# mLSTM as three rounded passes, rounded local-branch weights by casting transfers, and the gates' rows in the first branch gate's projection

## The chip, the core and the metric

The kernel runs on one core of a Trainium2 chip. A time is the device time of one launch in microseconds; the figure for a kernel is the median of its runs. Before the change it is 880.17 us, the median of three runs that lie between 879.93 and 880.27. The profile is that of one further execution, taken by the hardware profiler.

## The reference, cut to what matters

One decoder layer for 512 tokens of width 1024, all inputs float32. On one normalised input it computes an mLSTM branch (4 heads, keys of 128, values of 256) and a sliding-window attention branch ("local branch"), each multiplied by its own branch matrix, weighed by its own sigmoid gate and added; then an output projection, an MLP, a gated embedding and a last norm.

```python
proj = h @ w_in
qk_ml, v_ml, o_ml, if_pre, q_sw, k_sw, v_sw, g_a, g_b = jnp.split(proj, split_idx, axis=-1)
qk_ml = silu(causal_depthwise_conv(qk_ml, conv_qk))
...
log_d = where(causal, b[t] - b[s] + ic[s], -inf)      # b: running sum of the log forget gate
m_t = maximum(inter, max(log_d))
scores = einsum("bhtk,bhsk->bhts", qc, kc) * exp(log_d - m_t)
num = w_inter * (C @ qc) + einsum("bhts,bhsv->bhtv", scores, vc)
den = w_inter * (n @ qc) + sum(scores)
h = num / maximum(abs(den), exp(-m_t))
...
y_a = sigmoid(o_ml) * h_ml
merged = sigmoid(g_a) * (y_a @ w_branch_a) + sigmoid(g_b) * (y_b @ w_branch_b)
x = x + merged @ w_out
```

The kernel computes the mLSTM for the whole sequence at once: for a head it forms the 512 x 512 lower triangle of `scores` in 128 x 128 blocks (four key blocks `s`, four query blocks `t`, ten pairs with `s <= t`) and multiplies it by the values, with a column of ones beside the values so that the row sum `den` falls out of the same product.

## The kernel before, in words

TensorE (`T`, PE in the profile) is given float32 data in two ways. Most products are split: an operand `x` is rounded to float32r (`hi`, a copy on ScalarE, L137), the rest `x - hi` is subtracted on VectorE (`lo`, L138), and a product is three rounded passes, hi·hi, hi·lo and lo·hi (`pairs`, L163, issued by `chain`, L171). The products of the mLSTM are instead given plain float32 operands, one call each: `ml_scores` (L819) and `ml_out` (L831).

The stages around the change, in order of time in the profile:

- The v projection (`by_tokens(w_vml, ...)`, L530, about 44 to 83 us), then the o projection (L592, to about 123 us). Each is done by `seven` (L438), a form with seven products of quarter matrices instead of eight, whose results come out of PSUM by `post` under the names p1, c11, t21, t22, c22, c12, c21. `put_v` (L517) writes v, with a one in column 256 of each head, to the four `vm` tiles; `put_o` stores sigmoid(o) to DRAM (`god`, on POOL's queue).
- The gates' rows (L536 to L578): from the 8 gate preactivations of every token, as rows of 4 x 512, the running sums and maxima on VectorE with three activations on ScalarE (`lf`, `mst`, `fl`, `rr`, `gg`, `em`). `rr` is stored to DRAM (L554) and read back, one row per head broadcast over 128 partitions (`rows`, L565), both on POOL's queue; 14 small transposes on PE (L572, L574) turn `gg` and `em` into columns, which five copies bring to `gc`. In the program all this stands between the v and the o projection.
- The two branch gates (`gate_proj`, L596; w_gb about 123 to 165 us, w_ga to about 204 us), each as two halves `j`, each half by `seven`; results go to DRAM (`gd`) on POOL's queue. The remaining q, the mLSTM's q and k (`qk_proj`, `silu`) and the attention (`swa_probs`, `swa_out`) follow, to about 325 us.
- The mLSTM itself (about 325 to 400 us): for each head `ml_decay` (exponentials on ScalarE), `ml_scores`, `ml_out`, `ml_norm`; between them `branch_b(i)`, eight products of 24 matmuls with the weights `w_b`, and at the end `ya_of`, transposes and splits into the `ya` tiles. Then `merge` multiplies `ya` by `w_a`.

A weight is loaded raw by a transfer on SP's queue (L152), then rounded and subtracted (`load_w`, L155); `wh` and `wl` have four buffers each. Tiles of one tag share a fixed number of buffers: 34 of 512 columns ("act"), two of the big form that `h`, `ya` and `x1` take one after the other ("big"), four of 1024 columns ("lm"). The order of the instructions of each engine is not the written order: a planner places an instruction when its inputs and buffers are there by its own model of the costs, and takes the one written first where several could go. `tc.issue_after(x)` keeps what follows behind instruction `x`.

Of the kernel before, what the change touches and what calls it, by code (L numbers as in the profile page):

```python
# [16 lines left out]
P = 128  # L17
S = 512
# [18 lines left out]
def block_kernel(  # L37
# [82 lines left out]
    def tk(n):  # L120
        return tp_.tile([P, NH * (DV + 1)], F32, tag="tk", bufs=4, name=nm(n))
# [33 lines left out]
    def load_w(src, n, dims, raw=None):  # L155
# [4 lines left out]
        split(parts, raw[:, :n])  # L160
        return [q.rearrange("p (k c) -> p k c", k=dims) for q in parts]
# [317 lines left out]
    for m in range(NT):  # L479
        t = tk("vm").rearrange("p (h d) -> p h d", h=NH)  # L480
        G.memset(t[:, :, DV : DV + 1], 1.0)
        vm.append(t)

# [32 lines left out]

    def put_v(m, nh, ps, k):  # L517
        o = vm[m][:, 2 * nh : 2 * nh + 2, :DV]
        src = ps.rearrange("p (h d) -> p h d", h=2)
# [10 lines left out]
    by_tokens(w_vml, post_by_tokens(put_v), True)  # L530

# [8 lines left out]
    lf = row("lf")[:4, :]  # L540
    V.scalar_tensor_tensor(lf, fg, -1.0, fg, ALU.mult, ALU.max)
    A.activation(lf, lf, AF.Exp, scale=-1.0)
    A.activation(lf, lf, AF.Ln, bias=1.0)
    V.scalar_tensor_tensor(lf, fg, 0.0, lf, ALU.min, ALU.subtract)
    mst = act_f("mst")[:4, :]
    V.tensor_tensor_scan(mst, lf, ig, 0.0, ALU.add, ALU.max)
    fl = row("fl")[:4, :]
    for c in range(NT):
        V.tensor_tensor_scan(fl[:, c * P : (c + 1) * P], lf[:, c * P : (c + 1) * P], zeros4, 0.0, ALU.add, ALU.add)
    rr = act_f("rr")[:4, :]  # L550
    V.tensor_sub(rr, fl, mst)

    rrd = dp.tile([NH, 512], F32, name="rrd")
    nc.gpsimd.dma_start(out=rrd, in_=rr)  # L554
    gg = [act_f("gg")[:4, :] for _ in range(NT)]
    for t in range(NT):
        sl = slice(t * P, (t + 1) * P)
        V.tensor_sub(gg[t][:, sl], ig[:, sl], fl[:, sl])
        if t:
            V.tensor_scalar_add(gg[t][:, : t * P], gg[t - 1][:, : t * P], fl[:, t * P - 1 : t * P])  # L560
    em = act_f("em")[:4, :]
    A.activation(em, mst, AF.Exp, scale=-1.0)
    rows = [row("row") for _ in range(NH)]
    for h in range(NH):
        nc.gpsimd.dma_start(out=rows[h], in_=rrd[h : h + 1, :].broadcast_to([P, 512]))  # L565

    pgc = pg[:, :512]
    with tc.issue_after(last_mm[0].ins):
        for t in range(NT):
            for s in range(t + 1):  # L570
                c = (t * NT + s) * 4
                T.transpose(pgc[:, c : c + 4], gg[t][:, s * P : (s + 1) * P], ident[:4, :4])  # L572
            c = (NT * NT + t) * 4
            T.transpose(pgc[:, c : c + 4], em[:, t * P : (t + 1) * P], ident[:4, :4])  # L574
    gc = c1.tile([P, NT * NT + NT, 4], F32, name="gc")
    for t in range(NT):
        V.tensor_copy(gc[:, t * NT : t * NT + t + 1, :], pgc[:, t * NT * 4 : (t * NT + t + 1) * 4].rearrange("p (a b) -> p a b", b=4))
    V.tensor_copy(gc[:, NT * NT :, :], pgc[:, NT * NT * 4 : (NT * NT + NT) * 4].rearrange("p (a b) -> p a b", b=4))  # L578


# [15 lines left out]
    def gate_proj(wd):  # L596

        out_d = [None] * 4
        for j in range(2):
# [21 lines left out]
            def post(what, ps):  # L621
                new = lambda: act_f(what).rearrange("p (n c) -> p n c", n=2)
                if what == "p1":
                    keep["p1"] = new()
                    A.copy(keep["p1"], ps)  # L625
                elif what[0] == "t":
                    keep[what] = new()
                    add(keep[what], ps, keep["p1"])
                else:
                    half, nh = int(what[1]), int(what[2]) - 1  # L630
                    o = res[nh][:, :, 256:] if half == 1 else res[nh][:, :, :256]
                    if what != "c11":
# [3 lines left out]
                    A.activation(o, ps, AF.Sigmoid)  # L636
# [17 lines left out]
    gbd = gate_proj(w_gb)  # L654
# [118 lines left out]
    qk_proj(7)  # L773

    for h in range(NH):
        silu(h)
        silu(4 + h)


# [8 lines left out]
    def ml_decay(h):  # L788
        pr = rows[h]
        dg = act_f("dg")  # L790
        V.tensor_tensor(
            dg.rearrange("p (t j) -> p t j", t=NT),
            pr.rearrange("p (t j) -> p t j", t=NT),
            tri.unsqueeze(1).broadcast_to([P, NT, P]),
            ALU.add,
        )
        wT = []
        for s in range(NT):
            dm = act_f("dm")
            for t in range(s, NT):  # L800
                src = dg if t == s else pr
                A.activation(
                    dm[:, t * P : (t + 1) * P],
                    src[:, t * P : (t + 1) * P],
                    AF.Exp,
                    bias=gc[:, t * NT + s, h : h + 1],
                )
            wT.append(dm)
        wts[h] = wT

    def ml_scores(h):

        two, one = ps_a(), ps_t()
        banks = [two[:, :512], two[:, 512:], one, two[:, 512:]]
        at = [0, 0, 0, 384]
        for s in (0, 1, 3, 2):
            n0 = s * P
            psc = banks[s][:, at[s] : at[s] + S - n0]
            T.matmul(psc, qk[4 + h][:, n0 : n0 + P], qk[h][:, n0:], start=True, stop=True, skip_group_check=True)  # L819
        for s in range(NT):  # L820
            n0 = s * P
            dm = wts[h][s]
            V.tensor_mul(dm[:, n0:], banks[s][:, at[s] : at[s] + S - n0], dm[:, n0:])

    def ml_out(h):
        wT = wts.pop(h)
        for half in (1, 0):
            pn = ps_a().rearrange("p (n c) -> p n c", n=2)
            for t in (2 * half, 2 * half + 1):
                for s in range(t + 1):  # L830
                    last_mm[0] = T.matmul(  # L831
                        pn[:, t % 2, : DV + 1], wT[s][:, t * P : (t + 1) * P], vm[s][:, h, :], start=s == 0, stop=s == t, skip_group_check=True
                    )
# [26 lines left out]
    def branch_b(i):  # L860
        ps = ps_g()
        mm_T(ps, load_w(w_b[i], KT * P, KT), yb)
# [3 lines left out]

    _, ya = big_hl("ya")
# [24 lines left out]
    for h in range(NH):  # L892
        branch_b(NH + h)
        ya_of(h)

# [542 lines left out]
```

## Time and profile before

| | |
|---|---|
| median of three runs | 880.17 us |
| the profiled execution | 879.82 us, with a span of 878.0 us |
| instructions in the span | 11545, of them 4372 matmuls |
| granted TensorE clock | 0.998 of full |
| HBM | 91.30 MB read, 8.40 MB written |
| transfers | SP's queue 93.15 MB, POOL's queue 12.59 MB |

Busy times are sums of an engine's instructions. Matmuls overlap in the pipeline, so the mean length of one in a group (389 ns at 512 columns) is longer than the step from one to the next; a step is read from the chain of waits, which gives the time of so many matmuls in a row. In a group, "out<-in" names the tiles, and the shape is partitions x elements. "wr", "wh", "wl" are weights raw, rounded and rest; "ps.." are PSUM tiles; "SPq" and "POOLq" are the sequencers that issue transfers.

### The profile page before, as it was taken

Reading aid. Unit: us, or ns where it says so; the run is one execution under the profiler, and the core shown is the slowest. Engines: PE = TensorE matmul, PEld = TensorE weight load, DVE = VectorE, ACT = ScalarE, POOL = GpSimd, SP = SyncE. Lnnn points to the kernel's source line nnn. Section 1 sums busy time; section 2 is a strip of 40 time slices with the busy share of each in tenths; the row PEclk is TensorE's granted clock in tenths of the full one; section 3 lists DMA queues with packets and bytes.
Section 4 is the critical chain, followed back from the end, with each engine's and each line's share of the span. In section 5 each row is a group of like instructions: output and inputs, shape, how many; then the busy total and the mean of one; then the engine's idle time right before and its main releaser. Section 6 shows DMA issues by size and latency. Waiting matters only on the chain.

```text
span 878.0 us, 11545 instructions
## 1 busy us (share of the span) xinstructions
PE 866.8 (99%) x4372; PEld 725.6 (83%) x4372; DVE 657.2 (75%) x966; ACT 483.5 (55%) x803; POOL 34.1 (4%) x58
## 2 busy tenths in 40 slices
PE   8999999999999999999999999999999999999996
PEld 7888889998777777788888888888888888888886
DVE  6999887875789876665896669756956794698557
ACT  6684554544676768743344665356435634564843
POOL 1111010000000000000020000000000000020000
PEclk9999999999999999999999999999999999999999
DMA  7765244435122162274244612530352054125302
GB/s 266 211 180 186 73 150 169 165 111 196 52 73 72 49 199 88 97 240 144 72 75 145 236 49 71 197 106 10 124 185 75 1 186 149 49 52 141 121 0 96
DMA packets 32793, 106.74 MB, mean 122 GB/s; under 512 B 4573, under 2 KB 4573, under 8 KB 32738
## 3 DMA queue, kind: packets, MB, share of 16 engines
q1 hardware_dynamic: 27570, 93.15, 31.2%
q0 software_dynamic: 5024, 12.59, 5.9%
q8 instruction: 34, 0.56, 0.3%
q10 hardware_dynamic: 144, 0.26, 0.1%
q14 instruction: 21, 0.17, 0.1%
HBM read 91.30 MB, written 8.40 MB: 114 GB/s over the span
## 4 chain that ended last, share of the span: by engine, by line
PE 90%; DVE 4%; ACT 3%; DMA 2%; issue 1%; SPq 0%; ACTq 0%; DVEq 0%
PE psg L171 50%; PE psp L171 23%; PE psa L171 7%; PE pst L171 4%; PE psa L831 1%; PE pst L747 1%; DVE wl L138 1%; DMA wr<-in_w_vsif 1%; ACT lm L712 1%; PE psa L819 1%; PE psa L689 1%; PE psa L690 1%; ACT wh L137 0%; DMA wr<-in_w_gb 0%; PE psp L980 0%
## 5 line engine op out<-in xcount | busy, mean ns | idle before, releaser
L137 ACT CAST wh<-wr 128x1024 fp32r<-128x1024 f32 x138 | 144.8, 1051 | 180.3 <-PE psg L171 74.8
L138 DVE TENSOR_TENSOR wl<-wr,wh 128x1024 fp32r<-128x1024 f32 x138 | 167.8, 1219 | 85.9 <-ACT wh L137 84.6
L171 PE MATMUL psg<-x,wh 128*128 128x512 f32 x512 | 157.7, 389 | 0.0
L171 PE MATMUL psp<-wh,uf 128*128 128x512 f32 x448 | 138.6, 389 | 0.0
L171 PEld LDWEIGHTS psg<-x,wh 128*128 128x128 f32 x512 | 96.0, 188 | 19.9
L171 PE MATMUL psg<-x,wl 128*128 128x512 f32 x256 | 99.6, 389 | 0.0
L171 PEld LDWEIGHTS psp<-wh,uf 128*128 128x128 f32 x448 | 84.1, 188 | 17.5
L171 PE MATMUL psp<-wl,uf 128*128 128x512 f32 x224 | 87.2, 389 | 0.0
L171 PE MATMUL psg<-h,wh 128*128 128x512 f32 x256 | 81.1, 395 | 0.7 <-DVE rc L715 0.7
L137 ACT CAST wh<-wd 128x1024 fp32r<-128x1024 f32 x44 | 46.2, 1052 | 54.0 <-PE psp L171 21.9
L138 DVE TENSOR_TENSOR wl<-wd,wh 128x1024 fp32r<-128x1024 f32 x44 | 53.1, 1217 | 14.7 <-ACT wh L137 14.5
L171 PEld LDWEIGHTS psg<-x,wl 128*128 128x128 f32 x256 | 48.0, 188 | 10.0
L171 PEld LDWEIGHTS psg<-h,wh 128*128 128x128 f32 x256 | 47.0, 188 | 11.2 <-issue 1.6
L171 PE MATMUL psg<-h,wl 128*128 128x512 f32 x128 | 50.5, 395 | 0.0
L138 DVE TENSOR_TENSOR uf<-F,uf 128x1792 fp32r<-128x1792 f32 (+2 forms) x20 | 33.0, 1652 | 21.8 <-ACT uf L137 21.8
L171 PEld LDWEIGHTS psp<-wl,uf 128*128 128x128 f32 x224 | 42.0, 188 | 8.7
L171 PE MATMUL psg<-yb,wh 128*128 128x512 f32 x128 | 41.3, 402 | 0.1
L171 PE MATMUL psg<-ya,wh 128*128 128x512 f32 x128 | 39.5, 390 | 0.0
L137 ACT CAST uf<-F 128x1792 fp32r<-128x1792 f32 (+2 forms) x20 | 27.9, 1396 | 20.5 <-DVE F L1133 20.4
L1157 DVE SCALAR_TENSOR_TENSOR xk<-psp,r,xk 128x512 f32<-128x512 f32 x48 | 33.7, 744 | 5.5 <-PE psp L171 5.2
L171 PE MATMUL psg<-hS,wh 128*128 128x256 f32 x192 | 35.6, 284 | 0.0
L171 PE MATMUL psa<-h,wh 128*128 128x256 f32 x192 | 35.3, 285 | 0.2 <-ACT p L625 0.2
(322 smaller groups left out, 1745.6 us busy)
## 6 DMA issues: line engine op xcount, KB each, us to landing
wr<-in_w_up SPq DMA_DIRECT2D x32, 512.0 KB, 3.3
wd<-in_w_down SPq DMA_DIRECT2D x24, 512.0 KB, 3.7
wr<-in_w_qsw SPq DMA_DIRECT2D x8, 512.0 KB, 4.3
gd<-gr POOLq DMA_DIRECT2D x8, 512.0 KB, 3.7
wr<-in_w_qkml SPq DMA_DIRECT2D x8, 512.0 KB, 3.2
wr<-in_w_b SPq DMA_DIRECT2D x8, 512.0 KB, 3.2
gl<-gd SPq DMA_DIRECT2D x8, 512.0 KB, 3.4
wr<-in_w_a SPq DMA_DIRECT2D x8, 512.0 KB, 4.4
```

The source lines that it names most:

```text
L137: A.copy(dst[0], src)
L138: last_low[0] = V.tensor_sub(dst[1], src, r32(dst[0]))
L171: last_mm[0] = T.matmul(ps, l, r, start=first and i == 0, stop=last and i == len(ops) - 1, skip_group_check=parts)
L689: T.matmul(o, q[:, n * P : (n + 1) * P], kk[kp][ab][:, k0 : k0 + 256], start=True, stop=False)
L690: T.matmul(o, q[:, n * P : (n + 1) * P], kl[kp][ab][:, k0 : k0 + 256], start=False, stop=True)
L712: A.activation(lm3[:, g, :], lm3[:, g, :], AF.Exp, bias=nmx[:, g : g + 1], scale=0.125, accum_out=sm[:, g : g + 1])
L747: T.matmul(o[HALF[ab], :], v[:, c : c + 64], w[:, ab * 512 : (ab + 1) * 512], start=j == 0, stop=j == len(terms) - 1)
L819: T.matmul(psc, qk[4 + h][:, n0 : n0 + P], qk[h][:, n0:], start=True, stop=True, skip_group_check=True)
L831: last_mm[0] = T.matmul(pn[:, t % 2, : DV + 1], wT[s][:, t * P : (t + 1) * P], vm[s][:, h, :], start=s == 0, stop=s == t, skip_group_check ...
L1157: V.scalar_tensor_tensor(o, ps[:, t, :], r2[:, 2 * toks + t : 2 * toks + t + 1], o, ALU.mult, ALU.add)
```

## The change

In the mLSTM every product becomes three rounded passes. `vm` holds rounded v, with two columns of ones per head (258 columns); the rest of v goes to DRAM (`vld`, eight stores on POOL's queue) and is read back per head on SP's queue. q and k of a head and its weights `wT` are split on ScalarE and VectorE into the slots of the `ya` tiles, taken in turn (`spare`). Scores of the last key block are computed over 256 columns, of which 128 are used. The 128 x 512 tiles of weights per head become three of 512, 384 and 256 + 128 columns. `ya`'s tiles are taken earlier, and head 0's decay is written ahead of `qk_proj(7)`. The eight branch products stand two ahead of head 0's outputs, one ahead of each later head's, one between head 2's outputs and head 3's scores, and two at the end.

`branch_b` gets its rounded weights by a second transfer from DRAM that casts, on POOL's queue; the rest is still a subtraction on VectorE.

The gates' rows are computed in the first branch gate's projection: `gates` is called where the first half's t22 is read, `gate_columns` where the second half's c11 is read.

```diff
-        return tp_.tile([P, NH * (DV + 1)], F32, tag="tk", bufs=4, name=nm(n))
+        return tp_.tile([P, NH * (DV + 2)], F32, tag="tk", bufs=4, name=nm(n))
...
+        if cast:
+            nc.gpsimd.dma_start(out=parts[0], in_=src)
+            last_low[0] = V.tensor_sub(parts[1], raw[:, :n], r32(parts[0]))
+        else:
+            split(parts, raw[:, :n])
...
+        A.copy(t[:, :, DV:], ones[:, : 2 * NH].rearrange("p (h d) -> p h d", h=NH))
...
+    def store_low():
+        for o, t in kept:
+            nc.gpsimd.dma_start(out=o, in_=t)
+        kept.clear()
+
     def put_v(m, nh, ps, k):
+        if k is not None:
+            store_low()
         o = vm[m][:, 2 * nh : 2 * nh + 2, :DV]
+        two = lambda t: t.rearrange("p (h d) -> p h d", h=2)
+        low = act_r("vl")
         if k is None:
-            A.copy(o, src)
+            A.copy(o, two(ps))
+            V.tensor_sub(two(low), two(ps), r32(o))
         else:
-            V.tensor_add(o, src, k.rearrange("p (h d) -> p h d", h=2))
+            V.tensor_add(k, ps, k)
+            A.copy(o, two(k))
+            V.tensor_sub(two(low), two(k), r32(o))
+        kept.append((vld[:, 2 * nh : 2 * nh + 2, m, :], two(r32(low))))
...
+    def gates():
+        lf = row("lf")[:4, :]
...
+    def gate_columns():
+        pgc = ps_t()
...
             def post(what, ps):
+                for work in beside.pop((j, what), ()):
+                    work()
...
-    gbd = gate_proj(w_gb)
+    gbd = gate_proj(w_gb, {(0, "t22"): [gates], (1, "c11"): [gate_columns]})
...
+    ya_parts, ya = big_hl("ya")
+    def spare():
+        k = turn[0] % KT
+        turn[0] += 1
+        return [t[:, k, :] for t in ya_parts]
+    def qk_parts(h):
+        for i in (h, 4 + h):
+            hl = spare()
+            split(hl, qk[i])
+            qk[i] = hl
...
     def ml_scores(h):
+        psc = [two[:, :512], two[:, 512:896], one[:, :256], one[:, 256:]]
+        q, k = qk[h], qk[4 + h]
         for s in range(NT):
+            n0 = min(s, 2) * P
+            ops = pairs([t[:, s * P : (s + 1) * P] for t in k], [t[:, n0:] for t in q])
+            for j, (l, r) in enumerate(ops):
+                T.matmul(psc[s], l, r, start=j == 0, stop=j == 2, skip_group_check=True)
+        for j, n in enumerate((512, 384, 384)):
+            for s in ((0,), (1,), (2, 3))[j]:
+                V.tensor_mul(wT[s], psc[s][:, P:] if s == 3 else psc[s], wT[s])
+            hl.append([t[:, :n] for t in spare()])
+            split(hl[j], dm[j][:, :n])
...
     def ml_out(h):
+        low = sp.tile([P, NT, DV], F32R, tag="lm", bufs=LMB, name=nm("vl"))
+        nc.sync.dma_start(out=r32(low), in_=vld[:, h])
...
+                    T.matmul(o, hi, vm[s][:, h, :], start=s == 0, stop=False, skip_group_check=True)
+                    T.matmul(o[:, :DV], hi, low[:, s, :], start=False, stop=False, skip_group_check=True)
+                    last_mm[0] = T.matmul(o, lo, vm[s][:, h, :], start=False, stop=s == t, skip_group_check=True)
...
-        mm_T(ps, load_w(w_b[i], KT * P, KT), yb)
+        mm_T(ps, load_w(w_b[i], KT * P, KT, cast=True), yb)
...
     ml_decay(0)
+    qk_proj(7)
+    silu(0)
+    silu(4)
+    qk_parts(0)
     ml_scores(0)
+    for h in range(1, NH):
+        silu(h)
+        silu(4 + h)
     rds = []
+    todo = list(range(KT))
     for h in range(NH):
-        branch_b(h)
+        for _ in range(1 if h else 2):
+            branch_b(todo.pop(0))
         if h + 1 < NH:
             ml_decay(h + 1)
+            qk_parts(h + 1)
         with tc.issue_after(last_mm[0].ins):
             rds.append(ml_out(h))
         if h + 1 < NH:
+            if h == 2:
+                branch_b(todo.pop(0))
             with tc.issue_after(last_mm[0].ins):
                 ml_scores(h + 1)
...
     for h in range(NH):
-        branch_b(NH + h)
+        if h % 2 == 0:
+            branch_b(todo.pop(0))
         ya_of(h)
```

More of the change, by code (lines that the diff above doesn't have):

```diff
@@ L153, in load_raw, with load_w @@
         return raw
-    def load_w(src, n, dims, raw=None):
+    def load_w(src, n, dims, raw=None, cast=False):
         if raw is None:
@@ L530, in block_kernel @@
     by_tokens(w_vml, post_by_tokens(put_v), True)
+    store_low()
     def row(n):
@@ L539, in block_kernel @@
     V.tensor_copy(fg, pgf[:4, :])
[L540 to L578, printed above, removed]
     god = dp.tile([P, NH, NT, DV], F32, name="god")
@@ L771, in block_kernel @@
             swa_out(*units[u][:2])
[L773 to L777, printed above, removed]
+    ya_parts, ya = big_hl("ya")
+    turn = [0]
+    def spare():
[7 more added lines that the diff above has]
+            qk[i] = hl
     hs = [[act_f("hs") for _ in range(2)] for _ in range(NH)]
@@ L796, in ml_decay @@
         )
-        wT = []
+        dm = [act_f("dm") for _ in range(3)]
+        wT = [dm[0], dm[1][:, :384], dm[2][:, :256], dm[2][:, 256:384]]
         for s in range(NT):
-            dm = act_f("dm")
             for t in range(s, NT):
```

70 lines of the change are left out of this document (49 added, 21 removed).

## The prediction

> **What bounds the kernel now.** I read the page's busy shares first, then the chain of waits in order of time, then busy time by stretches.
>
> ```profile
> PE 866.8 (99%) x4372; PEld 725.6 (83%) x4372; DVE 657.2 (75%) x966; ACT 483.5 (55%) x803; POOL 34.1 (4%) x58
> PE 90%; DVE 4%; ACT 3%; DMA 2%; issue 1%; SPq 0%; ACTq 0%; DVEq 0%
> 60.00:95.00 35.00, 35.00 (x165) 28.69 (x164) 34.86 (x50) 19.71 (x22) 3.44 (x6) 1.00 0.51 170
> 95.00:128.00 33.00, 32.83 (x169) 28.03 (x168) 25.45 (x27) 17.36 (x21) 4.98 (x7) 1.00 0.36 128
> 128.00:165.00 37.00, 37.00 (x307) 36.69 (x306) 29.98 (x37) 17.44 (x21) 1.63 (x3) 1.00 0.43 152
> 165.00:204.00 39.00, 39.00 (x321) 38.48 (x320) 29.29 (x36) 19.47 (x24) 2.13 (x4) 1.00 0.44 155
> 325.00:400.00 75.00, 74.72 (x341) 60.44 (x340) 48.99 (x103) 51.93 (x116) 0.00 (x0) 1.00 0.44 148
> ```
>
> The last five rows give stretch, length, then busy time of PE, PEld, DVE, ACT and POOL, the granted clock, DMA share and GB/s. PE is busy throughout at full clock, and 90% of the chain is PE. So a pass of TensorE that disappears is worth its own length, unless an engine that feeds PE now comes late. Those feeders are loaded unevenly: VectorE is full from 60 to 95, where the v projection ends and the o projection begins (34.86 of 35.00 us), has 7.55 us free in the rest of the o projection, 7.0 in the first branch gate's, 26 in the mLSTM stretch.
>
> **The change part by part. First the PE passes.** These pieces of the chain (start, length, what, how many) price every form of matmul that the change touches:
>
> ```profile
> 357.85 4.33 PE psa L831 x20
> 366.75 1.72 PE psa L819 x6
> 362.19 0.43 PE pst L819 x2
> 133.70 2.88 PE psa L171 x24
> 21.28 5.79 PE psg L171 x48
> 386.88 5.46 PE psg L171 x24
> L831 PE MATMUL psa<-vm,dm 128*128 128x257 f32 x80 | 18.1, 380 | 0.0
> L171 PE MATMUL psg<-wh,h 128*128 128x264 f32 x64 | 13.0, 296 | 0.0
> ```
>
> The code multiplies 40 pairs of blocks at L831 and four per head at L819; the group shows 80, the chain 6 + 2 per head. An unrounded product is therefore two instructions: 4.33/20 = 0.217 us each at 257 columns. A rounded product is one: 2.88/24 = 0.120 us at 256 columns, 5.79/48 = 0.121 at 264, 5.46/24 = 0.228 at 512.
>
> Outputs: per head 10 pairs, now three instructions of 258, 256 and 258 columns, 30 x 0.121 = 3.62 us for 4.33. Scores: before 1.72 + 0.43 = 2.15 us per head. After, three passes over 512, 384, 256 and 256 columns (the last block is widened from 128). The 384-column rounded form is not in the trace; it lies between 0.120 and 0.228, and I take the midpoint 0.174, since cost grows evenly with columns between those rows. 3 x (0.228 + 0.174 + 0.120 + 0.120) = 1.93 us, by the ends 1.76 and 2.09. Saved: 0.71 + 0.22 = 0.93 us per head, **3.7 us for four heads** (3.1 to 4.4 by those ends).
>
> The Trainium skill, FP8 and Floating Point Precision, section TensorE Precision Notes, says that true FP32 takes four passes through the array. Read as three passes for four, 17.3 us of outputs would fall by 4.3 and 8.6 us of scores, with the wider block, by 1.5: 5.8 us, 874.4 as the time. The trace has each pass dearer when it is its own instruction (0.120 us against half of 0.217), so I keep 3.7.
>
> **Second, VectorE and ScalarE in the mLSTM.**
>
> ```profile
> L138 DVE TENSOR_TENSOR wl<-wr,wh 128x1024 fp32r<-128x1024 f32 x138 | 167.8, 1219 | 85.9 <-ACT wh L137 84.6 <-PE psg L171 0.8
> L137 ACT CAST wh<-wr 128x1024 fp32r<-128x1024 f32 x138 | 144.8, 1051 | 180.3 <-PE psg L171 74.8 <-PE psp L171 53.0 <-issue 20.9
> L138 DVE TENSOR_TENSOR ms<-ms,ms 128x512 fp32r<-128x512 f32 x8 | 5.3, 684 | 0.5 <-ACT ms L137 0.5
> L137 ACT CAST ms<-ms 128x512 fp32r<-128x512 f32 x8 | 4.8, 620 | 7.1 <-DVE ms L923 7.1
> L823 DVE TENSOR_TENSOR dm<-psa,dm 128x384 f32<-128x384 f32 x4 | 2.2, 550 | 0.2 <-ACT dm L802 0.2
> L676 DVE SCALAR_TENSOR_TENSOR acc<-acc,sg 128x512 f32<-128x512 f32 x8 | 5.0, 683 | 0.0
> 327.01 1.28 ACT L675
> 330.35 1.88 PE psg L171 x7
> 334.38 4.58 PE psg L171 x20
> 374.18 5.49 PE psg L171 x24
> PEld psa L819 <- DVE hd L835: 0.6, 1, 0.6
> ```
>
> Each head gets five new splits: q and k (512), and weights of 512, 384 and 384. VectorE: 3 x 0.684 + 2 x 0.550 = 3.15 us, 12.6 in all; ScalarE about 3 x 0.62 + 2 x 0.50 = 2.9 us, 11.4 in all, against 8 x 1.051 = 8.4 us of casts of `w_b` that go to transfers. Between 325 and 400 VectorE becomes 48.99 + 12.6 = 61.6 of 75 - 3.7 = 71.3 us (86%), ScalarE 51.93 + 3.0 = 54.9. Neither is full, so the cover is the eight products of `branch_b`, 5.46 us each, that PE runs between heads. The latency, though, grows: from a score to its use there is now a copy and a subtraction more, 0.62 + 0.68 = 1.3 us. Two heads get two products in front, two get one; with one product the 5.46 us must hold multiplications (1.9 us as before), splits (1.78 on VectorE), and other VectorE work. If the cover is gone the price is 1.3 us per head. The entry is tight as well: rounded q and k of head 0 go into slots of the normalised input's tiles, free only when `qk_proj(7)` has been read. The serial piece behind it is table load 1.28, two sigmoids, as long as a cast, and two products (0.683 each, together 2.6), splits (2.0), scores 1.9, products and splits of the weights (4.5): 12.3 us against two branch products and the scores, 2 x 5.46 + 1.9 = 12.8 us. Bounds: 0 to 4 x 1.3 = 5.2 us, or a gain of up to 0.6 us (a weight load of L819 that waited for an eviction, the last row above); taken 0.5. At the end two branch products, 10.9 us, still cover head 3's normalisation, which took 6.5 us from its last matmul (374.18) to its end (380.65, quoted below).
>
> **Third, transfers.**
>
> ```profile
> wr<-in_w_b SPq DMA_DIRECT2D x8, 512.0 KB, 3.2
> xk<-q POOLq DMA_DIRECT2D x6, 256.0 KB, 5.5
> god<-t POOLq DMA_DIRECT2D x4, 256.0 KB, 2.7
> 378.98 1.67 DVE L855 SCALAR_TENSOR_TENSOR hs<-hs,rs,og 128x256 f32<-128x256 f32 x4
> ```
>
> A casting load of 512 KB on POOL's queue is not in the trace. Bounds: 3.2 us (the plain load) and 2 x 5.5 = 11 us (twice the slowest computing transfer of half the size); taken 6. It starts when a `wh` buffer falls free, of four, so three other weights of at least 5.46 us each, 16 us, cover even 11 us plus the 1.22 us subtraction: cost 0; uncovered it would be 11 + 1.2 us once, since later loads overlap. POOL has no other work between 325 and 400. The eight stores of low v (256 KB, 2.7 us like the stores of o) stand in POOL's queue before the stores of o and have over 200 us until use. Four 512 KB loads on SP take scratch slots shared with `og`; low v of head 3 needs a slot freed by head 0's normalisation, two branch products earlier. Cost 0.
>
> The Trainium skill, SBUF — State Buffer, section Who interferes with whom, speaks against moving work to POOL's queue: a VectorE copy with both ports locks GpSimd out, and descriptors come late. Between 60 and 95, with VectorE 34.86 of 35.00 us busy, two row loads were issued in 1.10 us (below), so this trace shows no such starvation; by the rule a load would wait at most one VectorE instruction, inside the 16 us.
>
> **Fourth, the gates' rows.**
>
> ```profile
> 54.43 0.68 DVE L541 SCALAR_TENSOR_TENSOR lf<-fg 4x512 f32<-4x512 f32 x1
> 68.44 1.21 DVE L546 TENSOR_TENSOR_SCAN mst<-lf,ig 4x512 f32<-4x512 f32 x1
> 69.58 1.33 DVE L549 TENSOR_TENSOR_SCAN fl<-lf,zero 4x128 f32<-4x128 f32 x4
> 79.65 0.40 DVE L560 TENSOR_SCALAR gg<-gg,fl 4x384 f32<-4x384 f32 x1
> 84.59 0.37 DVE L577 COPY gc<-psa 128x4 f32<-128x4 f32 x4
> 75.78 1.10 POOL L565 DMA_DIRECT2D row<-rrd  x2 [2.31 <-DMA rrd<-rr]
> 142.07 0.55 POOL L641 DMA_DIRECT2D gd<-gr  x1 [15.72 <-ACT gr L636]
> 134.77 0.42 DVE L617 TENSOR_TENSOR t<-psg,p 128x256 f32<-128x256 f32 x1
> 136.42 0.40 PE L171 MATMUL psg<-hS,wh 128*128 128x256 f32 x2
> 150.96 1.22 DVE L138 TENSOR_TENSOR wl<-wr,wh 128x1024 fp32r<-128x1024 f32 x1 [3.12 <-ACT wh L137]
> ```
>
> The rows' VectorE work is three of 0.68 + 1.21 + 1.33 + about 2.0 for `gg` (seven instructions of up to 0.40) = 6.6 us, with 0.37 and one copy more, about 0.6, for the columns; ScalarE has three activations and three table loads, 3 x (0.63 + 1.28) = 5.7 us, and up to two more loads, since sigmoids of the gate stand between. All leave the full v projection, where eight subtractions of low v, 8 x 0.68 = 5.5 us, and six more copies on ScalarE come in: VectorE there stays level, cost 0. In the new place VectorE has 29.98 + 7.2 = 37.2 of 37.00 us: too much for that stretch alone, but the end of the o projection before it has 7.55 us free and the second gate 9.7 after. Rows ran in gaps among weights before (54.43 to 80), though written behind all of that stage's products; their inputs are ready at 54 us. The store of `rrd` and four row loads now pass behind the eight POOL stores of o and before the gate's own stores (the first at 142.07); behind those waits only `gd`, and its tiles are next wanted in the second gate, 20 us on. If the rows pack into the gate's first half, weights come up to 6.6 us late minus 3.1 us of idle (150.96) and about 1.2 us more: 2.4 us of stall. The 14 small transposes move unchanged. Bounds 0 to 9.2 us (last rival), taken 0.3, nearest to gap filling.
>
> **Sum.** The profiled execution took 879.82 us, span 878.0 and 1.8 around it; the median shown is 0.35 above. 879.82 - 3.7 + 0.5 + 0.3 = 876.9, beside the median 877.2.
>
> **The rivals.** (a) The splits' latency is exposed where one branch product stands in front and at the entry: three times 1.3 on top of nothing else, 880.2 - 3.7 + 3.9 = 880.4. For it: each of these steps crosses between two engines that are 77 and 86% busy by the sums above. Against: the branch products' matmuls already stand in pieces around the scores of head 0 (7 before them at 330.35, 20 after them at 334.38), so they move to where they are needed.
>
> (b) Slower: the rows block the first gate. In the program they stand ahead of the addition that empties Z (134.77), and Z's next product began at 136.42, 1.2 us after that addition ended. If VectorE's queue holds the rows there in written order, with two round trips through ScalarE, the addition is 6.6 + 2 x 1.91 = 10.4 us late, PE stalls 9.2, and the time is 885.7. From a delay of 1.2 + 3.7 + 1.8 = 6.7 us on, the kernel is slower by over 0.2%. Against: the rows stood in gaps before.
>
> (c) More gain: no new stall, the 0.6 us before L819 gone, and passes at the low end, 4.4: 875.2. The four-to-three rule, 874.4, belongs here with 0.03.
>
> **How the numbers follow.** The forecast 877.2 (876.4 to 878.4) has 0.48, (c) 0.12, (a) 0.18, (b) 0.22, of which a partial blocking of 6.7 to 9 us holds most. Faster by over 0.2% means under 878.4 (about what these runs can tell from no change): 0.48 + 0.12 and a little of (a), 0.62. Within: 0.17. Slower: 0.21. The range 874.4 to 884.5 leaves out the full price of (b) and little else; the likeliest case's own range stands above.
>
> **What would show it.** L831's successor at 3.6 us per head and L819's at 1.9; no PE gap over 1 us between 325 and 400 and none in 130 to 160; casting loads landing in under 11 us; the rows' scans lying in VectorE's gaps rather than in one block ahead of L617. A block of rows beside an idle PE near 135 makes (b) right; PE idle ahead of each head's outputs makes (a) right.

## The result, and the profile after

The changed kernel takes 878.39 us (median of 16 runs, 877.46 to 879.46) beside 880.09 for the kernel before (16 runs, 879.74 to 880.53): a ratio of 0.9981, 95% interval 0.9973 to 0.9989. That is 1.7 us faster, where 2.9 were forecast: the gain is real, since the interval ends below 1, but it is of the size (0.2%) that the prediction called about the limit of what can be told. The profiled execution took 878.13 us, with a span of 876.3.

The page of the changed kernel, busy times and chain, and then its windows (stretch, length, busy time of PE, PEld, DVE, ACT, POOL, granted clock, DMA share, GB/s):

```profile
PE 864.2 (99%) x4428; PEld 727.1 (83%) x4428; DVE 671.5 (77%) x994; ACT 490.4 (56%) x826; POOL 43.7 (5%) x70
PE 84%; DVE 7%; ACT 4%; DMA 3%; issue 2%; SPq 0%; ACTq 0%; DVEq 0%
```

```profile
60.00:95.00 35.00, 34.20 (x150) 27.65 (x149) 33.62 (x42) 21.02 (x26) 4.97 (x7) 1.00 0.54 201
95.00:128.00 33.00, 32.80 (x167) 27.75 (x165) 26.68 (x28) 17.36 (x21) 4.97 (x7) 1.00 0.37 128
128.00:165.00 37.00, 36.65 (x308) 36.09 (x307) 31.60 (x49) 20.15 (x24) 3.78 (x7) 1.00 0.50 172
325.00:400.00 75.00, 74.74 (x413) 63.82 (x409) 59.30 (x122) 53.68 (x122) 2.65 (x5) 1.00 0.65 226
```

PE's share of the chain (the work that ended last, followed back) fell from 90 to 84%, and PE, which was busy for all of 60 to 95 and of 128 to 165, now stands for 0.8 and 0.35 us there. VectorE runs 10.3 us more between 325 and 400. The waits of PE name what it stands for (total, times, longest):

```profile
PE psg L175 <- DVE rc L746: 0.6, 1, 0.6
PE pst L175 <- DVE wl L138: 0.5, 1, 0.5
PE psa L720 <- DVE lm L732: 0.5, 1, 0.5
PE psg L175 <- DVE t L515: 0.3, 1, 0.3
PE pst L919 <- DVE ya L141: 0.3, 1, 0.3
```

Waits for `rc` and `lm`, in the attention, stood there before too. New are `wl` in the o projection, `t` in the v projection and `ya` at the end of the mLSTM.

To see where time comes and goes, I set the start of the n-th matmul of a kernel against that of the n-th matmul of the kernel before, with the 14 small transposes of the gates' columns left out of the count. From 405 us on the count runs from the end, since the number of matmuls in the mLSTM differs. This is worked out from all matmuls of both traces, so no single row shows it. Kernels E1 to E10 are the experiments below.

```
us later than the kernel before, at          55     82    110    204    321    405    865
the changed kernel                         0.00   0.49   0.31   1.97   1.96  -1.65  -1.71
E1 rows back between v and o               0.00   0.51   5.14   5.19   5.15   1.54   1.57
E2 no casting transfers                    0.00   0.49  -0.26   1.95   1.96  -2.43  -2.43
E3 rows behind both gates                  0.00   0.50   0.22   0.32   0.32  -2.57  -2.57
E4 subtractions of low v on GpSimd         0.01   0.52   2.94   5.09   5.06   1.61   1.57
E5 E2 and E3 together                      0.01   0.50   0.23   0.24   0.16  -4.13  -4.17
E6 no low v                                0.01   0.10  -0.87   2.12   2.17  -6.37  -6.46
E7 kernel before, rows moved               0.01  -0.01  -0.98   1.10   1.12   1.14   1.15
E8 low v by transfers                      0.02   0.53   2.08   4.26   4.25   0.63   0.63
E9 E5 with the rows held back              0.00   0.52  -0.02  -0.04   0.79  -3.46  -3.47
E10 casting transfers for six of eight     0.00   0.50   0.74   2.59   2.58  -1.29  -1.28
```

The transposes themselves take about 1.0 us. Where they have moved out of the v projection, everything behind their old place (82 to 83 us) starts that much earlier until they come in their new one: E7's -0.98 at 110 is that alone. With it, the changed kernel loses 0.5 us in the v projection, 0.8 in the o projection (0.31 - 0.49 + 1.0), 0.65 in the first gate (1.97 - 0.31 - 1.0), nothing in the second gate and the attention, and gains 3.6 in the mLSTM (from 1.96 to -1.65). From there to the end nothing changes. The balance is -1.7, which is what the medians show.

A row of this table is one execution, and the rows show by themselves how far one execution can be trusted. Up to 204 us the changed kernel, E2 and E10 have the same instructions in the same order on PE, VectorE, ScalarE and GpSimd; yet they stand at 0.31, -0.26 and 0.74 at 110 us, and at 1.97, 1.95 and 2.59 at 204. A difference of that size between two rows can't be put down to an edit. The end of a row is the profiled execution's, and that was the shortest of the runs for E1 (881.48 us, median 883.36) and E8 (880.55, median 882.51).

VectorE's timeline of the changed kernel shows where the scatter in the o projection comes from (in brackets the wait before an instruction):

```profile
72.73 1.22 DVE L452 TENSOR_TENSOR wq<-wq,wq 128x1024 f32<-128x1024 f32 x1 [0.97 <-DMA wq<-in_w_o]
```

VectorE waits here for a raw weight of the o projection, a load of 512 KB, and from here to 104 us it has no further gap. The same wait is 0.38 us in E2, 0.87 in E3, 0.89 in E5 and 1.36 in E10; these kernels lose 0.25, 0.72, 0.73 and 1.24 us in the o projection, the changed kernel 0.82. In each the loss is the wait less about 0.15 us. So the loss there takes two things: a load that lands late, and behind it a VectorE so full, with six of the eight subtractions of low v, that it cannot catch up. In E7, which has no low v, the same wait is 0.58 us and PE loses nothing. Why the load lands later in one execution than in another, and whether the stores of low v have a part in it, is not shown.

### The profile page after: what moved, and what is told of

The parts are those of the page before. It is cut to its first block, busy times and chain, and to the rows that moved or that the text cites. A ratio compares the mean times of both kernels' runs of the same rounds, so it can differ in the third digit from the quotient of the medians.

```text
span 876.3 us, 11735 instructions
## 1 busy us (share of the span) xinstructions
PE 864.2 (99%) x4428; PEld 727.1 (83%) x4428; DVE 671.5 (77%) x994; ACT 490.4 (56%) x826; POOL 43.7 (5%) x70
## 4 chain that ended last, share of the span: by engine, by line
PE 84%; DVE 7%; ACT 4%; DMA 3%; issue 2%; SPq 0%; ACTq 0%; DVEq 0%
PE psg L175 47%; PE psp L175 23%; PE psa L175 5%; DVE wl L138 2%; PE pst L175 2%; PE pst L778 1%; ACT wh L137 1%; DMA wr<-in_w_vsif 1%; DMA wq<-in_w_o 1%; ACT lm L743 1%; PE psa L720 1%; PE psa L859 1%; PE psa L881 1%; DVE qs L429 1%; PE psa L879 1%
## 5 line engine op out<-in xcount | busy, mean ns | idle before, releaser
L137 ACT CAST wh<-wr 128x1024 fp32r<-128x1024 f32 x130 | 136.5, 1052 | 159.4 <-PE psg L175 61.7
L138 DVE TENSOR_TENSOR wl<-wr,wh 128x1024 fp32r<-128x1024 f32 x130 | 158.1, 1219 | 79.9 <-ACT wh L137 78.9
```

Source lines behind the costliest of these rows:

```text
L137: A.copy(dst[0], src)
L138: last_low[0] = V.tensor_sub(dst[1], src, r32(dst[0]))
```

## The gain: the passes

The chain of waits of the changed kernel from 325 to 402 (start, length, what, how many) has the new steps of PE:

```profile
364.89 0.12 PE psa L879
365.01 0.12 PE psa L880
...
371.77 1.20 PE psa L859 x6
372.97 0.72 PE pst L859 x6
```

A pass of the outputs steps at 0.12 us, so a head has 30 x 0.12 = 3.6; a head's scores take 1.20 + 0.72 = 1.92. Both are the prediction's numbers (3.62 and 1.93). The new VectorE work per head has its rows too, and they are those that the prediction took from other tiles:

```profile
L138 DVE TENSOR_TENSOR ya<-acc,ya 128x512 fp32r<-128x512 f32 x8 | 5.3, 684 | 0.0
L138 DVE TENSOR_TENSOR ya<-dm,ya 128x384 fp32r<-128x384 f32 x8 | 4.2, 550 | 0.0
```

## The experiments: what the v and o projections and the rows cost

**E1: the rows and their transposes back between the v and the o projection.** All else as in the changed kernel.

```diff
     V.tensor_copy(fg, pgf[:4, :])
+    gates()
+    gate_columns()
...
-    gbd = gate_proj(w_gb, {(0, "t22"): [gates], (1, "c11"): [gate_columns]})
+    gbd = gate_proj(w_gb)
```

> The changed kernel with the gates' rows and columns where they stood before, between the v and the o projection. Theory A (the loss of about 1.3 us in the v and o projections comes from VectorE, which low v's eight subtractions make late there; the loss of about 0.65 us in the first gate comes from the rows): 6.6 us of rows on top of low v in the stretch that is full, so PE comes out of the o projection 2 us or more later than before instead of about 1.3, the first gate loses nothing, time 879 to 881. Rival B (the move of the rows cost more than low v): 878 or less.

Measured: 883.36 us (881.48 to 883.79), ratio to the kernel before 1.0032, 1.002 to 1.0043. PE's waits in it:

```profile
PE psa L602 <- DVE gg L584: 1.9, 1, 1.9
PE psa L604 <- ACT em L588: 0.9, 1, 0.9
```

The transposes stand in PE's queue and wait for rows that VectorE, full, brings late. In the table all of the loss but the 0.5 us of the v projection falls between 82 and 110; the first gate then loses nothing. So the move is worth 5.0 us by the medians and 3.3 by the profiled executions, once low v is formed in the v projection: without it the change is slower than the kernel before. The direction was theory A's; the size was larger than it said.

**E7: the move alone, in the kernel before.** v, mLSTM and weights as they were.

```diff
-    gbd = gate_proj(w_gb)
+    gbd = gate_proj(w_gb, {(0, "t22"): [gates], (1, "c11"): [gate_columns]})
...
```

> The kernel before with the move of the rows alone; v, the mLSTM and the weights as before. Theory A (the move pays only because low v fills VectorE in the v projection; by itself it brings the first gate's loss of 0.3 to 0.7 us and no gain, as the rows lay in gaps there): 880.1 + 0.5 = 880.6 us, with PE waiting some 0.3 us for the additions of the gate. Rival I (the rows cost PE something in the v and o projections before too, and the move gives it back): 879.4 us, with the n-th matmul at 100 us earlier than before's.

Measured: 880.66 us (880.12 to 881.8), ratio 1.0009, 1.0000 to 1.0018. Theory A's 880.6. Its windows:

```profile
60.00:110.00 50.00, 50.00 (x222) 40.98 (x221) 42.67 (x48) 25.33 (x28) 1.48 (x2) 1.00 0.38 129
110.00:165.00 55.00, 54.68 (x412) 51.95 (x411) 46.84 (x65) 30.01 (x37) 8.57 (x14) 1.00 0.48 165
```

VectorE has 42.67 of 50 us where the rows are gone, and PE gains nothing from it: it was busy all of that stretch before. The rows' VectorE time in the v projection had cost nothing; moved, they cost 1.1 us in the two gates (-0.98 to 1.10, less the transposes' 1.0).

**E6: no low v at all.**

```diff
-        low = act_r("vl")
...
-            V.tensor_sub(two(low), two(k), r32(o))
-        kept.append((vld[:, 2 * nh : 2 * nh + 2, m, :], two(r32(low))))
...
-                    T.matmul(o[:, :DV], hi, low[:, s, :], start=False, stop=False, skip_group_check=True)
```

> Leaves out the low part of v: no subtractions, stores and loads of it, and the outputs have two passes for three. 40 passes of 0.121 us, 4.8 us, go in any case. Theory A (the loss of 1.3 us in the v and o projections comes from VectorE, full there, and the eight subtractions of low v): the loss falls to 0.3 or less, the n-th matmul at 100 us starts within 0.3 us of before's, and the time is 878.4 - 4.8 - 1.0 = 872.6 us. Rival H (the loss is of the six rounding copies on ScalarE, or of the rows' work still there, both of which stay): it stays at 1.3, and the time is 873.6 us.

Measured: 873.16 us (872.0 to 873.59), ratio 0.992, 0.9906 to 0.9934. The total lies between the two theories; the table separates them. At 82 us the loss is 0.1, and at 110 it is -0.87 + 1.0 = 0.1: the loss of 1.3 us is gone, as theory A says, and all kernels with low v lose 0.7 or more up to there. The run takes out the stores of low v together with its subtractions; that the subtractions count is read from VectorE's timelines, which have no gap from 73.9 to 104 us in the changed kernel and are idle for 1.7 us at 95 here. But the gates lose 2.0 us (-0.87 to 2.12, less 1.0) instead of 0.65, or 1.2 in E2. VectorE's and PE's timelines of this kernel (start, length, instruction, with its wait):

```profile
138.46 0.76 DVE L642 TENSOR_TENSOR t<-psg,p 128x256 f32<-128x256 f32 x2 [1.27 <-ACT em L600]
```

```profile
138.94 0.51 PE L175 MATMUL psg<-hS,wh 128*128 128x256 f32 x2 [1.17 <-DVE t L642]
```

The addition that empties Z waits for `em`, which is no input of it, so presumably for a tile that comes free when `em` is formed; PE stands for 1.17 us. That is rival (b) of the prediction, the rows in front of that addition, at an eighth of its price.

**E3: the rows behind both gates.**

```diff
-    gbd = gate_proj(w_gb, {(0, "t22"): [gates], (1, "c11"): [gate_columns]})
+    gbd = gate_proj(w_gb)
     gad = gate_proj(w_ga)
+    gates()
     for i in range(1, 4):
         q_proj(i)
+    gate_columns()
```

> The changed kernel with the gates' rows written behind both branch gates, beside the projections of q, and the columns behind those. Theory A: the first gate gets back its 0.65 us less the waits that it had before (about 0.2), nothing else moves: 877.6 to 878.0. Rival B (rows still go into gaps of the v projection and are what makes it late): the loss in v and o goes too, 876.5 or less. Rival D (rows are not what the gate waits for): 878.4.

Measured: 877.23 us (876.33 to 879.27), ratio 0.9971, 0.9961 to 0.9982, 1.2 us better than the changed kernel and below theory A's 877.6 to 878.0. The v and o projections lose what they did, so rival B is out. At 204 us, with the transposes still to come, it stands at 0.32: the gates lose nothing more. The transposes then come in during the attention and the offset stays, because the waits for `rc` and `lm` (1.1 us in the changed kernel) are no longer in this kernel's list. Some of this is given back in the mLSTM, which gains 2.9 instead of 3.6; E2 shows why.

**E4: six of the eight subtractions of low v on GpSimd.**

```diff
-            V.tensor_sub(two(low), two(k), r32(o))
+            G.tensor_sub(two(low), two(k), r32(o))
```

> The changed kernel with six of the eight subtractions of low v (those with both operands in SBUF) on GpSimd instead of VectorE. Theory A: 4.1 us less on VectorE between 73 and 88 us, the o projection loses 0.2 us instead of 0.85, the 0.44 us at 60 stays: 877.5 to 877.9. Rival E (the o projection is late for its raw weights, which share the transfers with low v's stores): 878.4. Rival F (GpSimd's reads hold VectorE up): 878.5 or more.

Measured: 882.05 us (881.46 to 883.18), ratio 1.0023, 1.0014 to 1.0032: 3.7 us worse than the changed kernel, as rival F has it. The groups of this kernel from 60 to 110 us, against 1.2 us for VectorE's 1024 columns elsewhere:

```profile
L541 POOL TENSOR_TENSOR vl<-t,vm 128x512 fp32r<-128x512 f32 x4 | 6.5, 1618 | 19.1 <-ACT vm L540 19.1
L453 DVE TENSOR_TENSOR wr<-wq,wr 128x1024 f32<-128x1024 f32 x2 | 3.5, 1767 | 0.0
L462 DVE TENSOR_TENSOR wr<-wr,wr 128x1024 f32<-128x1024 f32 x2 | 3.4, 1708 | 0.0
```

While GpSimd subtracts, VectorE's own instructions of this size take 1.7 us for 1.2, and single ones more; its timeline has one of the longest:

```profile
90.94 2.33 DVE L138 TENSOR_TENSOR wl<-wr,wh 128x1024 fp32r<-128x1024 f32 x1
```

Summed over the seven that run beside GpSimd's six, VectorE takes some 5 us longer. The window of 60 to 110 us in this kernel, and then in the changed one:

```profile
60.00:110.00 50.00, 47.22 (x204) 37.71 (x203) 45.76 (x47) 27.34 (x32) 14.71 (x14) 1.00 0.47 172
```

```profile
60.00:110.00 50.00, 49.20 (x216) 39.87 (x215) 45.65 (x54) 28.51 (x33) 5.69 (x8) 1.00 0.47 173
```

VectorE is busy for as long, 45.76 and 45.65 us, although 6 x 0.68 = 4.1 us of subtractions have left it, and PE is busy for 2 us less. GpSimd's subtraction is itself 1.2 to 2.0 us long. The Trainium skill, SBUF — State Buffer, section Who interferes with whom, says that a VectorE instruction with two inputs in SBUF contends with a GpSimd instruction that reads SBUF; the trace agrees, with the 1.7 against 1.2 us above.

**E8: six of the eight by ScalarE and a transfer.** The rest of v as a negated rounding to which a transfer on POOL's queue adds v.

```diff
-            V.tensor_sub(two(low), two(k), r32(o))
+            A.activation(low, k, AF.Copy, scale=-1.0)
+            G.dma_start(out=r32(low), in_=k, accum_op=ALU.add)
```

> The low part of v of six of eight tiles is formed by a negated rounding on ScalarE and a transfer that adds v to it, in place of VectorE's subtraction. Theory A (VectorE's time is what the v and o projections lack): 6 x 0.68 = 4.1 us less of it, the loss of 1.3 us falls to some 0.4, and the time is 877.5 us. Rival J (ScalarE's six more instructions of 0.62 us, or six transfers of 256 KB that hold tiles and POOL's queue, take its place): 878.4 us or more, with PE waiting for ScalarE's roundings between 60 and 110 us.

Measured: 882.51 us (880.55 to 884.62), ratio 1.0029, 1.0018 to 1.004. Rival J. Its waits from 55 to 115 us:

```profile
ACT vl L541 <- DMA vl<-t: 3.2, 1, 3.2
PE pst L175 <- ACT p L512: 2.2, 1, 2.2
```

ScalarE waits 3.2 us for a transfer that still holds a tile, and behind it in ScalarE's order stands the eviction `p` (a copy out of PSUM) that PE waits for. The run does not separate this wait from ScalarE's six added instructions of 0.63 us. Less VectorE work does not help if another engine is blocked in its place.

**E9: the rows kept out of the v projection altogether**, on top of E5 below. In the changed kernel the planner had drawn the first of the rows' work forward (shortest, median and longest in ns, first and last start):

```profile
L586 DVE SCALAR_TENSOR_TENSOR lf<-fg,lf x1: 671/671/671, 67.6 to 67.6; 4x512 f32<-4x512 f32 x1
L591 DVE TENSOR_TENSOR_SCAN fl<-lf,zero x4: 385/386/408, 69.3 to 70.3; 4x128 f32<-4x128 f32 x4
```

```diff
+        with tc.issue_after(last_low[0].ins):
             V.scalar_tensor_tensor(lf, fg, -1.0, fg, ALU.mult, ALU.max)
```

> The kernel with both single edits (weights of branch_b rounded on ScalarE, rows behind both gates; 875.9 us), and the rows' first instruction held on VectorE until the low weights formed before it in the program are done, so that none of the rows' work can be planned forward into the v projection, where the first parts still lie (one of 0.67 us at 67.6 and four of 0.39 us from 69.3 us). Theory A (every us of VectorE's time in the full stretch is late weight): 2.2 us less there, the stall at 88 us shrinks or goes, and the time is 875.3 us. Rival K (what is late there is a chain of dependent steps, not VectorE's sum): the stall stays, and the rows, now in one piece beside q_proj and the attention, cost as much there: 875.9 to 876.5 us.

Measured: 876.93 us (876.03 to 878.88), ratio 0.9968, 0.9959 to 0.9977, 1.1 us worse than E5 (0.7 in the profiled executions). VectorE's timeline shows what became of the 2.0 us that it has less to do in its full stretch:

```profile
70.54 1.23 DVE L138 TENSOR_TENSOR wl<-wr,wh 128x1024 fp32r<-128x1024 f32 x1 [1.50 <-ACT wh L137]
72.39 1.23 DVE L452 TENSOR_TENSOR wq<-wq,wq 128x1024 f32<-128x1024 f32 x1 [0.63 <-DMA wq<-in_w_o]
```

It is idle instead, and then waits for the same load of the o projection as before, 0.63 us for E5's 0.89. The o projection loses 0.46 us (-0.02 - 0.52 + 1.0) for E5's 0.73, again the wait less 0.15 or so, and no more apart than executions of one program are. Work taken from VectorE ahead of that load gives nothing back that these traces can show. The rows came in one piece,

```profile
203.70 1.21 DVE L589 TENSOR_TENSOR_SCAN mst<-lf,ig 4x512 f32<-4x512 f32 x1
...
208.68 0.40 DVE L603 TENSOR_SCALAR gg<-gg,fl 4x384 f32<-4x384 f32 x1
```

just ahead of the attention. There this kernel goes from -0.04 to 0.79, with the transposes in and the wait for `rc`, 0.7 us, back, where E5 stays level. As far as these traces tell, rival K was right: the stall hangs on a chain of steps, here that load, and not on VectorE's sum ahead of it, and the rows cost more in their new place. The median is 0.4 us above its range.

## The experiments: what the casting transfers cost

**E2: the weights of `branch_b` rounded on ScalarE again.**

```diff
-        mm_T(ps, load_w(w_b[i], KT * P, KT, cast=True), yb)
+        mm_T(ps, load_w(w_b[i], KT * P, KT), yb)
```

> The changed kernel with w_b's rounded weights cast on ScalarE again, no casting transfers. Theory A (the cover of the branch products hides ScalarE; the casts are worth little): ScalarE 53.7 + 8.4 = 62 us of the 71 of the mLSTM stretch, PE loses at most 0.6 us more there, time 878.4 to 879.2. Rival C (without the transfers ScalarE becomes the bound of the mLSTM): 880 or more, with PE waiting for ScalarE in front of scores and outputs.

Measured: 877.48 us (876.94 to 877.86), ratio 0.997, 0.9959 to 0.9982, 0.9 us better than the changed kernel and below both theories, neither of which had the casting transfers cost anything. The mLSTM gains 4.4 us (1.96 to -2.43) instead of 3.6, so the casting transfers, meant to unload ScalarE, cost some 0.75. Set against E2 matmul by matmul, the changed kernel loses this in two steps, 0.38 us at 356.6 and 0.37 at 391. The transfers themselves are quick; the rows of issues of the changed kernel (count, size, median us to landing):

```profile
wh<-in_w_b POOLq DMA_DIRECT2D x8, 512.0 KB, 3.7
vld<-vl POOLq DMA_DIRECT2D x8, 256.0 KB, 2.8
```

But a load starts only when PE has let go of a `wh`, and lands 3.7 us later, where ScalarE needs 1.05 from the same point. POOL's timeline of the changed kernel, and VectorE's:

```profile
351.39 0.53 POOL L161 DMA_DIRECT2D wh<-in_w_b  x1 [10.51 <-PE psg L175]
```

```profile
354.96 1.22 DVE L162 TENSOR_TENSOR wl<-wr,wh 128x1024 fp32r<-128x1024 f32 x1 [1.84 <-DMA wh<-in_w_b]
356.10 0.42 DVE L864 TENSOR_TENSOR dm<-pst,dm 128x256 f32<-128x256 f32 x1
356.43 0.15 DVE L883 COPY hd<-psa 128x2 f32<-128x2 f32 x1
```

VectorE stands for 1.84 us at the subtraction of a weight that PE does not need yet, and what PE does need (`dm`, and `hd`, which empties PSUM) is queued behind it. The weight load of PE's next scores waits for `hd`; the timeline of PEld (PE's weight loads) in the changed kernel:

```profile
356.63 0.19 PEld L859 LDWEIGHTS psa<-ya 128*128 128x128 f32 x1 [0.43 <-DVE hd L883]
```

In E3 the same wait is longer and PE's next scores are late by it; E3's VectorE and E3's waits of PE:

```profile
353.91 1.23 DVE L162 TENSOR_TENSOR wl<-wr,wh 128x1024 fp32r<-128x1024 f32 x1 [2.85 <-DMA wh<-in_w_b]
```

```profile
PE psa L861 <- DVE hd L885: 0.8, 1, 0.8
```

The second half of the cost is at the end of the mLSTM. VectorE of the changed kernel, then of E2:

```profile
389.76 1.21 DVE L138 TENSOR_TENSOR wl<-wr,wh 128x1024 fp32r<-128x1024 f32 x1
390.89 1.40 DVE L141 SCALAR_TENSOR_TENSOR ya<-pst,gml,ya 128x512 fp32r<-128x512 f32 x2
```

```profile
389.39 1.40 DVE L141 SCALAR_TENSOR_TENSOR ya<-pst,gml,ya 128x512 fp32r<-128x512 f32 x2
390.71 1.22 DVE L138 TENSOR_TENSOR wl<-wr,wh 128x1024 fp32r<-128x1024 f32 x1
```

With casting transfers the planner puts a weight of the merge ahead of `ya`, and the transposes behind wait for `ya`; in E2 it is the other way round, and PE's wait is gone from its list; PE's weight loads there wait 0.3 us for `ya` instead of 1.0.

**E10: casting transfers for six of the eight weights.**

```diff
-        mm_T(ps, load_w(w_b[i], KT * P, KT, cast=True), yb)
+        mm_T(ps, load_w(w_b[i], KT * P, KT, cast=i < 6), yb)
```

> The changed kernel with casting transfers for the first six weights of branch_b, and ScalarE for the last two. Theory A (what the casting transfers cost is VectorE's order at the end of the mLSTM: weights whose high part is there early are subtracted ahead of the last heads' splits and of ya, and the transposes behind wait 0.4 us): the wait of the transposes at 391 us goes, and the time is that of the kernel without casting transfers or a little above, 877.5 to 877.9 us. Rival L (the cost lies in the loads themselves, 4 MB more of transfers beside the mLSTM's own): it falls by a quarter only, 878.2 us.

Measured: 878.38 us (877.77 to 879.19), ratio 0.9981, 0.9972 to 0.999. The wait at the end is still there:

```profile
PE pst L919 <- DVE ya L141: 0.3, 1, 0.3
```

and the mLSTM gains 3.9 (2.58 to -1.29), a quarter of a us more than with eight; the step at 356.6 shrank, the one at 391 did not. So theory A falls in so far as the last two weights do not decide the order at the end. It comes out of the planner's whole sequence; which of the six tips it stays open. The median is that of the changed kernel (878.38 and 878.39), and rival L's 878.2 is too near to it for these runs to tell. Its reason, the traffic of the loads, is not shown.

**E5: E2 and E3 together.**

> Both single edits at once: the weights of branch_b rounded on ScalarE again, and the gates' rows behind both branch gates. Theory A (each of the two parts has a price of its own, at another place: 0.9 us for the casting transfers, in the mLSTM; 1.2 us for the rows, in the first gate and the attention): they add up, 878.4 - 0.9 - 1.2 = 876.3 us. Rival G (both edits remove the same slack, some late weight, and only one of the gains can be had): 877.2 us, like the better of the two alone.

Measured: 875.86 us (875.27 to 876.72), ratio to the kernel before 0.9956, 0.9942 to 0.9969: 4.0 us faster than before and 2.5 faster than the change. It is the best of all kernels with the reference's whole computation. The two gains add up, so rival G is out. It is 0.4 us better than their sum (876.3), which lies within its five runs; the traces give a reason for it, since with the rows late the casting transfers had cost more: the mLSTM gains 4.3 here and 2.9 in E3. PE's longest waits from 20 to 410 us:

```profile
PE pst L175 <- DVE wl L138: 0.4, 1, 0.4
PE psg L175 <- DVE t L515: 0.3, 1, 0.3
```

What is left is the loss in the v and o projections; two more waits of 0.2 us stood in the kernel before too.

## Why the prediction was right, and where it was not

The forecast, faster by 2.9 us through fewer passes, holds in sign and in its main term; four smaller terms were off, and these took 1.2 us of it. Forecast: -3.7 + 0.5 + 0 + 0 + 0.3, for passes, splits, transfers, v projection and rows. Measured: -4.3 (passes and splits) + 0.75 + 1.3 + 0.65 = -1.6, beside -1.7 by the medians. That 878.39 still lies within 876.4 to 878.4, by 0.01 us, is luck: the costs came to 2.7 us where 0.8 were set down, and 0.6 us of gain that the sum did not have made up for a part. The upper end of that range is also the line that the prediction drew for a gain of over 0.2%.

- **Passes, -3.7.** Right, with the steps of 0.12 and 1.92 us above. The reading of the Trainium skill's rule (FP8 and Floating Point Precision, section TensorE Precision Notes) as four passes for three, with its 874.4 us, is not borne out: an unrounded product is two steps of 0.217 us and a rounded one three of 0.12, a ratio of 3.6 to 3.
- **Latency of the splits, 0.5.** Too high. Without casting transfers the mLSTM gains 4.25 to 4.4 us (E5, E9, E2), so the splits cost nothing and some 0.6 more came. The wait of a weight load for `hd`, 0.6 us in the kernel before, is no longer among E2's waits; that it makes up the whole 0.6, as rival (c) had it, was not tried. Rival (a) is out: the branch products in front of each head do cover.
- **Transfers, "cost 0".** The step that failed is the cover. "Three other weights of at least 5.46 us each, 16 us, cover even 11 us" counts PE's stock of weights; it does not ask what stands behind the waiting subtraction on VectorE. The landing, 3.7 us, was inside the bounds, and the price was 0.75.
- **v projection, "VectorE there stays level, cost 0".** The largest miss, 1.3 us in the v and o projections. VectorE's sum did stay level: 33.62 us busy between 60 and 95, for 34.86 before. What failed was to take the sum for the price. It set 6.6 us of rows out against 5.5 us of subtractions in. E7 shows that the rows' time there had been free, since nothing near waited for them; E6 shows that low v's is not. Its subtractions stand in one order with the additions that empty PSUM and with the weights of the o projection, which PE wants next, and behind the load at 72.7 us VectorE has no gap left. So the size of the o projection's part, 0.25 to 1.24 us, goes by when that load lands. Also 2.0 us of the rows stayed, drawn forward by the planner; E9 shows that these cost nothing that the traces can tell. The move was needed all the same: without it E1 is 3.3 to 5.0 us slower.
- **Rows in the first gate, 0.3.** The place was right, the size 0.65 in the changed kernel's execution (0.85 in E10, 1.2 in E2, with the same instructions up to there). They filled gaps in part only; VectorE of the changed kernel:

```profile
129.76 0.43 DVE L646 TENSOR_TENSOR t<-psg,p 128x256 f32<-128x256 f32 x1 [0.18 <-PE psg L175]
130.10 1.20 DVE L588 TENSOR_TENSOR_SCAN mst<-lf,ig 4x512 f32<-4x512 f32 x1
131.23 1.19 DVE L138 TENSOR_TENSOR wl<-wr,wh 128x1024 fp32r<-128x1024 f32 x1
132.35 0.41 DVE L646 TENSOR_TENSOR t<-psg,p 128x256 f32<-128x256 f32 x1
```

The scan `mst` and a weight come between the two halves of the addition that empties Z, and PE's next product waits for the second half. The prediction had named no gap of PE between 130 and 160 as its sign; there is one of 0.37 us at 132.4. Rival (b) is the right mechanism far below its price of 9.2: the round trips through ScalarE were done before this place, except `em`.

## What to carry to other kernels

VectorE time moved out of a full stretch is not exchanged one for one with time moved in: ask of each instruction whether anything near waits for it, since late work that nobody wants costs nothing and a subtraction in front of a PSUM eviction costs at once. Ask also on which side of the next wait it stands: here 2.0 us taken out ahead of a load became idle time, while 4.1 us put in behind it left no room to make up for the load. Before a difference of a tenth of a per cent is put down to an edit, compare executions of the same instructions: here they differ by 1 us in one stage. When a transfer takes the place of a copy, its latency begins where the buffer comes free, and it is paid by whatever is queued behind the first instruction that waits for it, not by the engine that was unloaded. And when an edit bundles a gain with several moves, test each alone: here one of the three parts (the casting) cost time, and another (the rows) was needed but stood in the second best place.

## What the hardware showed that was not expected

GpSimd subtractions held up VectorE's instructions on fp32 tiles by 0.5 to 1.1 us each, 1.7 to 2.3 us for 1.2, so that moving 4.1 us of work off VectorE left it busy for as long (E4). The transfers on POOL's queue were not longer for VectorE being full: the eight stores of low v landed in 2.8 us, the stores of o in the kernel before in 2.5 to 2.7. A load of 512 KB for the o projection made VectorE wait between 0.38 and 1.36 us in executions of the same instructions, and the o projection's loss followed it.
